# Modulation weights asked for three steps ahead, sums of squares as column strips, and the rotary key's tile two places earlier

## The chip, the cores and the metric

The kernel runs on one core of a Trainium2 chip. The metric is the device time of one execution in microseconds (us); several executions are timed, and the median is compared.

## The reference, cut to what matters

One decoder layer over 1024 tokens of width 1024 in float32: six modulation vectors from a condition vector, an input projection, latent attention beside a gated recurrence, an output projection, and a routed expert network of 32 experts. What the change touches is the modulation and the three latents of the input projection.

```python
mod = jax.nn.silu(c) @ w_ada + b_ada                      # 1024 -> 6 * 1024
shift1, scale1, gate1, shift2, scale2, gate2 = jnp.split(mod[:, None, :], 6, axis=-1)
h = rms_norm(x, norm1_g) * (1.0 + scale1) + shift1
proj = h @ w_in
q_lat, kv_lat, k_rope, x_lru, g_lru = jnp.split(proj, IN_SPLITS, axis=-1)
attn = mla_attention(q_lat, kv_lat, k_rope, ...)          # rms_norm(q_lat) @ w_q_b, rms_norm(kv_lat) @ w_kv_b
lru = rg_lru_branch(x_lru, g_lru, ...)                    # conv, two gates, a scan, times gelu(g_lru)
mixed = jnp.concatenate([rms_norm(attn, ...), rms_norm(lru, ...)], axis=-1)
x = x + gate1 * (mixed @ w_out)
h2 = rms_norm(x, norm2_g) * (1.0 + scale2) + shift2
x = x + gate2 * hierarchical_moe(h2, ...)
```

## The kernel before

The program is one stream that a scheduler orders at build time: engines take their instructions in the order that its timeline gives, and the code fixes pieces of that order with added dependencies (`ordered`, `add_manual_dep`). Each engine and each DMA queue then works strictly in its own order. SP is the queue of nearly all loads.

Big tiles come from one pool: tag `b` (`blk`, 128x1024, 41 slots) and tag `h` (`half`, 128x512, 12 slots). A load is issued when its slot is free, and everything behind it on SP waits with it.

The front of the layer runs to about 250 us. `FT` (L50) lists the twelve column tiles of the input projection: `kl` and `ql` are the latents, `xl` the recurrence's input, `kr` the rotary key, `gl` the gelu branch. Each tile's weights are split into a high and a low part, and each product is three matmuls (L225, L226, L227) of 128x512 into a bank `pp` (three banks); a `kr` tile has 64 columns, and both parts side by side, in two matmuls (L537, L538). The first three tiles (`k1` is 3) run half by half while the rows of x are normed and turned (L376, tiles `pt`, then `xT` on ACT, `hTh` and `hTl`); the others follow one by one. After a tile's half, `evac` takes the bank: `lat_k` and `lat_q` copy a latent and call `sq_cols` (L600), `conv` makes four ACT and DVE steps, `k_rope` sums the squares of the rotary key and turns it. `gate_mm` and `gate` (L563, L573) make the two gates of an `xl` tile, with tables changed on ACT between sigmoid, exp, tanh and sqrt.

`sq_cols` squares a half (128 features x 512 tokens, `sqq`) on ACT, and TensorE sums over the features: each 128 columns of `sqq` are the stationary operand and a column of ones the moving one (L605, 128x1), so that tokens land on partitions (`pc`), and DVE copies four columns into `ssq`.

`ada` (L483) makes the four later modulation vectors in sixteen steps, eight for each of two groups: a step loads 128 rows of `w_ada` as four tiles `wad` of 128x512 (L490) and runs four matmuls of 32x512 (L494), which stand on four strips of 32 columns of the array. The first of the four waits for all four loads, and the four stay together. After eight steps the bias is loaded (`adab`), added to the bank `pm`, and the result goes to DRAM (`mod_d`, L512) and from there to `m_g1`, with which POOL scales `wo`. The steps are handed out between the tiles of the projection (`next(ag)` after each four products). `modulate` (L439) does the same for the first two vectors, from 128x256 tiles (L445), at the start.

From there on attention runs head by head (to about 500 us), then the router and the experts, whose weights `ew` are 186 loads of 512 KB, issued as slots come free.

Of the kernel before, what the change touches and what calls it, by code (L numbers as in the profile page):

```python
# [14 lines left out]
AF = mybir.ActivationFunctionType  # L15
# [5 lines left out]
D = 1024  # L21
S = 1024
NT = 8
# [22 lines left out]
for _n, _w in ROWS:  # L46
    ROFF[_n] = (_o, _w)
    _o += _w
NROW = _o
FT = [("kl", 0), ("ql", 0), ("xl", 0), ("ql", 1), ("xl", 1), ("xl", 2), ("xl", 3), ("kr", 0),  # L50
      ("gl", 0), ("gl", 1), ("gl", 2), ("gl", 3)]
GE = 8
FRONT = [8 * g + i for i in range(2) for g in range(4)]
# [47 lines left out]
for _n, _w in GRP:  # L101
# [2 lines left out]
NGRP = _o  # L104
OPT = {
# [33 lines left out]
def layer(ctx, tc, A, out, dbg=None, stop=None):  # L139
    nc = tc.nc  # L140
    V, SC, G, T, SY = nc.vector, nc.scalar, nc.gpsimd, nc.tensor, nc.sync
# [8 lines left out]
    def blk(name, dt=F32):  # L150
        return big.tile([128, 1024], dt, name=name, tag="b", bufs=NBLK)

    def half(name, dt=F32):
        return big.tile([128, 512], dt, name=name, tag="h", bufs=NHALF)
# [11 lines left out]
    def bank(name):  # L166
        ph = OPT["ph"][cur["n"]]
        tg = ph["tags"][name]
        return cur["ps"].tile([128, 512], F32, name=name, tag=tg, bufs=ph["n"][tg])
# [59 lines left out]
    def t3(ap, t):  # L229
        return ap.rearrange("p (t f) -> p t f", t=t)  # L230
# [5 lines left out]
    xs, last = {}, {}  # L236
# [9 lines left out]
    def load_in(i):  # L246
        if i >= len(FT):
            return
        kind, j = FT[i]
        M = 64 if kind == "kr" else 128  # L250
        f0 = FCOL[kind] + j * 128
        w = blk("win")
        v = t3(w, 8)[:, :, :M]
        SY.dma_start(v, A["w_in"][:, f0:f0 + M].rearrange("(k p) f -> p k f", p=128))
        wraw[i] = v
# [64 lines left out]
    ones_f = const.tile([128, 128], F32, name="ones_f")  # L320
# [3 lines left out]
    ident = const.tile([128, 128], F32, name="ident")  # L324
# [11 lines left out]
    ones_c = ones_f[:, 0:1]  # L336
# [9 lines left out]
    cs32 = const.tile([128, 8, 32], F32, name="cs32")  # L346
# [134 lines left out]
    mc = {g: const.tile([128, 16], F32, name=f"mc{g}") for g in (1, 2)}  # L481

    def ada():  # L483
        for g in (1, 2):
            pm = bank("pm")
            for k in range(8):
                ws, ld = [], []
                for i in range(4):
                    w = half("wad")
                    ld.append(SY.dma_start(w, A["w_ada"][k * 128:(k + 1) * 128, g * 2048 + i * 512:g * 2048 + (i + 1) * 512]).ins)  # L490
                    ws.append(w)
                with ordered(T):
                    for i in range(4):
                        m = T.matmul(pm[32 * i:32 * i + 32, :], cs32[:, k, :], ws[i], start=(k == 0), stop=(k == 7),  # L494
                                     skip_group_check=True).ins
                        if i == 0:
                            for d in ld[1:]:
                                tc.add_manual_dep(m, d.name, mybir.DependencyInfo(
                                    mybir.DependencyClass.Sync, mybir.DependencyReason.DATA), reason="four at once")
                yield  # L500
            bt = half("adab")
            for i in range(4):
                b = A["b_ada"]
                SY.dma_start(bt[32 * i:32 * i + 32, :],
                             bass.AP(tensor=b.tensor, offset=b.offset + g * 2048 + i * 512, ap=[[0, 32], [1, 512]]))
            V.tensor_add(bt, bt, pm)
            pmc = bank("pmc")
            for c in range(4):
                T.matmul(pmc[:, c:16:4], bt[:, c * 128:(c + 1) * 128], ident[:, 0:128:32], start=True, stop=True)
            V.tensor_copy(mc[g], pmc[:, :16])  # L510
            for i in range(4):
                G.dma_start(mod_d[g * 2048 + i * 512:g * 2048 + (i + 1) * 512], bt[32 * i:32 * i + 1, :])  # L512
# [83 lines left out]
    ssq = const.tile([128, 3, NT], F32, name="ssq")  # L596
# [3 lines left out]
    def sq_cols(pp, n, j):  # L600
        sq = half("sqq")
        SC.activation(sq, pp, AF.Square)
        pc = bank("pc")
        for t in range(4):
            T.matmul(pc[:, t:t + 1], sq[:, t * 128:(t + 1) * 128], ones_c, start=True, stop=True)  # L605
        V.tensor_copy(ssq[:, j, n * 4:n * 4 + 4], pc[:, :4])

    def lat_q(i, n):
        j = FT[i][1]
# [21 lines left out]
    def k_rope(i, n):  # L631
        pp = hold.pop(i)
        if n == 0:
            lq["kr"] = blk("krT")
        kr = lq["kr"]
        SC.activation(kr[:, NS[n]], pp, AF.Copy)
        if n == 1:
            i2 = half("ident2")[:, :64]
            V.tensor_add(i2, ident[:, :64], ident[:, 64:])
            pk = bank("pk")  # L640
            for t in range(NT):
                T.matmul(pk[:, t * 64:(t + 1) * 64], kr[:, t * 128:(t + 1) * 128], i2, start=True, stop=True)
            kb = blk("kb")
            sqr, tmp = t3(kb[:, :512], NT), t3(kb[:, 512:], NT)
            with tc.issue_after(last["hi"]):
                SC.activation(sqr, t3(pk, NT), AF.Square)
            V.tensor_reduce(ssr, sqr, op=OP.add, axis=AX.X)
            rope(krr, t3(pk, NT), NT, "k", 0, tmp)

# [17 lines left out]
    ag = ada()  # L667
# [40 lines left out]
    lx, le, ld, l2, lp = (const.tile([128, 4], F32, name=n) for n in ("lx", "le", "ld", "l2", "lp"))  # L708
# [23 lines left out]
    SY.dma_start(rsti, bass.AP(tensor=A["pos_r"].tensor, offset=A["pos_r"].offset, ap=[[0, 128], [1, S]]))  # L732
    load_in(K1)
    load_in(K1 + 1)
    for i in range(8):
        kind, j = FT[i]
        if i >= K1:
            load_in(i + 2)
            split_in(i + 1)
            if i == 7:  # L740
                split_in(i + 2)
        if kind == "xl":
            load_gate(j)
        for n in range(2) if i >= K1 else (1,):
            for _ in project(i, n) if i >= K1 else ():
                for _ in range(OPT["adv"]):
                    next(ag, None)
            if n == (0 if i >= K1 else 1):
                gates()
            if (i, n) == (7, 1):  # L750
                wk = blk("wk")
                SY.dma_start(wk, A["w_kv_b"])
                wkh, wkl = blk("wkh", F32R), blk("wkl", F32R)
                last["hi"] = SC.activation(wkh, wk, AF.Copy).ins
                V.tensor_sub(wkl, wk, wkh)
            evac(i, n)
        if i < K1:
            wsp.pop(i)
        if i == 1:
            split_in(K1)  # L760
            V.tensor_scalar(rst, rsti, 0, None, op0=OP.is_equal)
            V.tensor_scalar(rcap, rst, -1.0, 2.0, op0=OP.mult, op1=OP.add)
        if kind == "xl":
            pend.append(j)
# [913 lines left out]
    for n, u in enumerate(UNITS):  # L1678
# [14 lines left out]
        pg = gate_up(u, X.pop(n), mid)  # L1693
# [81 lines left out]
```

## Time and profile before

| | us |
|---|---|
| median of 3 runs | 809.95 (808.85 to 810.82) |
| the profiled execution's own time | 816.49 |
| its span, first to last instruction | 814.6 |
| TensorE busy | 728.1 (89%) |
| VectorE busy | 447.2 (55%) |
| ScalarE busy | 317.0 (39%) |
| GpSimd busy | 157.6 (19%) |

The profiled execution is 6.5 us above the median, and what lies around its span is 1.9 us. Shares of the whole span mix stages with different limits: up to 500 us TensorE is busy nearly all the time and the DMA engines about half of it, and behind that it is the DMA engines that are full. A wait that TensorE has in the front is therefore read from the front alone.

### The profile page before, as it was taken

What the parts mean: (1) busy time and instruction counts of PE and PEld (TensorE: products, weight loads), DVE (VectorE), ACT (ScalarE), POOL (GpSimd) and SP (SyncE); (2) the same over time, 40 slices, a digit from 0 to 9 for tenths busy, and PEclk for the clock granted to TensorE, in tenths of its full rate; (3) what the DMA queues carried; (4) which work ended last, traced back from release to release, by engine and by line L of the source; (5) the groups of instructions that cost most, each with busy time, mean ns of one, the idle gap of its engine ahead of it and who ended that gap; (6) DMA issues with size and microseconds to landing.
All of it is one profiled execution on the core that took longest, in us unless ns stands there. A gap on an engine that the chain in (4) does not pass through costs nothing. (4 is left out here: it accounts for less than half of the span.)

```text
span 814.6 us, 12260 instructions
## 1 busy us (share of the span) xinstructions
PE 728.1 (89%) x4257; PEld 471.2 (58%) x4257; DVE 447.2 (55%) x1334; ACT 317.0 (39%) x715; POOL 157.6 (19%) x150
## 2 busy tenths in 40 slices
PE   3899999989988989899999997699979899999874
PEld 1477776548877878788888886333333343332321
DVE  4597386868777469797884667344334222213210
ACT  3455456666354157667664434121201211102200
POOL 1121012103665102031311000212112112212010
PEclk9989999999999999999999998699989999999998
DMA  9952437681317403020154789999999999999994
GB/s 311 372 151 84 143 108 236 210 280 58 109 44 259 168 39 104 1 79 1 54 173 144 259 311 343 346 316 349 313 373 330 329 335 336 369 347 354 304 320 102
DMA packets 70976, 180.47 MB, mean 222 GB/s; under 512 B 8960, under 2 KB 22528, under 8 KB 70912
## 3 DMA queue, kind: packets, MB, share of 16 engines
q1 hardware_dynamic: 63328, 158.50, 55.1%
q0 software_dynamic: 7104, 21.00, 9.5%
q8 instruction: 34, 0.56, 0.3%
q10 hardware_dynamic: 480, 0.16, 0.2%
q14 instruction: 30, 0.25, 0.1%
HBM read 160.61 MB, written 22.95 MB: 225 GB/s over the span
## 5 line engine op out<-in xcount | busy, mean ns | idle before, releaser
L1649 PE MATMUL pgu<-ew,xeT 128*32 128x512 f32 (+1 forms) x928 | 163.4, 613 | 8.1 <-DMA ew<-in_w_e 7.3
L1649 PEld LDWEIGHTS pgu<-ew,xeT 128*32 128x32 f32 (+1 forms) x928 | 48.3, 121 | 99.4 <-issue 79.0
L1660 PE MATMUL py<-ew,hT 128*32 128x512 f32 (+1 forms) x464 | 75.1, 597 | 5.8 <-ACT hT L1634 5.8
L225 PE MATMUL pp<-hTh,winh 128*128 128x512 f32 x176 | 69.2, 406 | 5.8 <-DVE hTh L188 3.0
L226 PE MATMUL pp<-hTl,winh 128*128 128x512 f32 x176 | 71.1, 404 | 0.0
L227 PE MATMUL pp<-hTh,winl 128*128 128x512 f32 x176 | 70.4, 401 | 0.0
L1663 DVE TENSOR_TENSOR y<-py,m_g 128x512 f32<-128x512 f32 (+1 forms) x40 | 27.5, 691 | 69.3 <-PE py L1660 64.3
L1623 ACT ACTIVATE sg<-pgu 128x256 f32<-128x256 f32 (+1 forms) x20 | 7.7, 387 | 142.9 <-PE pgu L1649 135.8
L1660 PEld LDWEIGHTS py<-ew,hT 128*32 128x32 f32 (+1 forms) x464 | 23.5, 120 | 48.3 <-issue 35.7
L1616 DVE TENSOR_SCALAR xeT<-pxe,gc,mc 128x128 f32<-128x128 f32 x80 | 27.4, 404 | 33.0 <-PE pxe L1610 33.0
L225 PEld LDWEIGHTS pp<-hTh,winh 128*128 128x128 f32 x176 | 34.0, 194 | 16.3 <-DVE hTh L188 4.0
L1665 POOL DMA_INDIRECT out<-y,pki x13 | 20.7, 1589 | 111.2 <-DVE y L1663 87.7
L1625 DVE SCALAR_TENSOR_TENSOR hid<-sg,pkw,pgu 128x256 f32<-128x256 f32 (+1 forms) x13 | 6.2, 479 | 63.4 <-ACT sg L1623 60.9
L1634 ACT ACTIVATE hT<-pht 128x256 f32<-128x256 f32 (+1 forms) x20 | 7.6, 380 | 85.1 <-PE pht L1632 65.4
L1614 ACT ACTIVATE xeT<-pxe,mc,gc 128x128 f32<-128x128 f32 x80 | 30.0, 461 | 24.9 <-PE pxe L1610 24.9
L226 PEld LDWEIGHTS pp<-hTl,winh 128*128 128x128 f32 x176 | 33.9, 193 | 9.9 <-issue 2.1
L227 PEld LDWEIGHTS pp<-hTh,winl 128*128 128x128 f32 x176 | 34.1, 194 | 8.6 <-issue 1.7
L949 ACT ACTIVATE P<-pS,nb,scq 128x384 f32<-128x384 f32 (+2 forms) x48 | 32.3, 679 | 12.2 <-DVE nb L946 12.2
L983 PE MATMUL po<-PT,v 128*128 128x256 f32 (+1 forms) x160 | 35.8, 362 | 0.0
L1046 POOL TENSOR_TENSOR wo<-wo,m_g 128x256 f32<-128x256 f32 x32 | 28.2, 916 | 15.3 <-DMA wo<-in_w_out 15.3
L983 PEld LDWEIGHTS po<-PT,v 128*128 128x128 f32 x160 | 28.8, 191 | 2.9
L1610 PEld LDWEIGHTS pxe<-ident,xe 128*128 128x128 f32 x160 | 18.2, 145 | 20.7 <-issue 14.4
(424 smaller groups left out, 1613.6 us busy)
## 6 DMA issues: line engine op xcount, KB each, us to landing
ew<-in_w_e SPq DMA_DIRECT2D x186, 512.0 KB
wad<-in_w_ada SPq DMA_DIRECT2D x64, 256.0 KB
wada<-in_w_ada SPq DMA_DIRECT2D x16, 512.0 KB
win<-in_w_in SPq DMA_DIRECT2D x12, 512.0 KB
xt<-in_x SPq DMA_DIRECT2D x8, 512.0 KB
wo<-in_w_out SPq DMA_DIRECT2D x8, 512.0 KB
xr<-in_x SPq DMA_DIRECT2D x8, 512.0 KB
x_d<-xr SPq DMA_DIRECT2D x8, 512.0 KB
```

What stands on the lines that cost most here:

```text
L225: T.matmul(o, lhi, rhi, start=first, stop=False)
L226: T.matmul(o, lhi, rlo, start=False, stop=False)
L227: T.matmul(o, llo, rhi, start=False, stop=last)
L949: SC.activation(Pt[:, o:o + w], pss[ci], AF.Exp, scale=P["scq"][:, i:i + 1], bias=nb, accum_out=l[:, ci:ci + 1])
L983: T.matmul(po[:, o:], P["v"][:, js], PT[j // 4][:, j % 4, o:], start=(j == 0), stop=(j == nj - 1), skip_group_check=True)
L1046: EN[OPT["g1"]].tensor_mul(w[:, q:q + 256], w[:, q:q + 256], mrow["g1"][:, q:q + 256])
L1614: SC.activation(xT[a][:, c], pt[:, c], AF.Identity, scale=gc[:, k:k + 1], bias=sh2[:, k:k + 1])
L1616: last["dve"] = V.tensor_scalar(xT[a][:, c], pt[:, c], gc[:, k:k + 1], sh2[:, k:k + 1], op0=OP.mult, op1=OP.add).ins
L1649: T.matmul(pg[r], xT[k // 4][:, c + r.start:c + r.stop], w[k // 2][:, NS[k % 2]], start=(k == 0), stop=(k == 7), skip_group_check=True)
L1660: T.matmul(py[n][r], hT[:, a * 128 + r.start:a * 128 + r.stop], w[4 + a][:, NS[n]], start=(a == 0), stop=(a == 1), skip_group_check=True)
L1663: last["dve"] = V.tensor_mul(y[:rows, NS[n]], py[n][:rows], mrow["g2"][:rows, NS[n]]).ins
L1665: G.indirect_dma_start(out=out, out_offset=bass.IndirectOffsetOnAxis(ap=idx, axis=0), in_=y[r0:r0 + idx.shape[0]], in_offset=None, compute ...
```

## The change

Three edits, and the order that the scheduler then finds.

- `ada` loads a step's weights as two tiles of 128x1024 from tag `b` in place of four of 128x512 from tag `h`. Three steps are asked for at the start (a `next(ag)` ahead of the fourth tile), and each step asks for the step three behind it, after its matmuls. The matmuls are the same 64, on halves of the two tiles; the first of a step waits for both loads.
- `sq_cols` swaps the operands: 32 columns of ones are stationary and 128 columns of `sqq` move, four times, on four strips of the array, so that a strip holds 32 equal rows of sums for 128 tokens. ACT copies the bank to `sqr`, TensorE transposes it (bank `pct`, of the two banks E), and DVE takes every 32nd column.
- In `FT` the `kr` tile stands sixth, ahead of the last two `xl` tiles, and its square on ACT has no order set any more.

```diff
@@ -47,7 +47,7 @@
     ROFF[_n] = (_o, _w)
     _o += _w
 NROW = _o
-FT = [("kl", 0), ("ql", 0), ("xl", 0), ("ql", 1), ("xl", 1), ("xl", 2), ("xl", 3), ("kr", 0),
+FT = [("kl", 0), ("ql", 0), ("xl", 0), ("ql", 1), ("xl", 1), ("kr", 0), ("xl", 2), ("xl", 3),
       ("gl", 0), ("gl", 1), ("gl", 2), ("gl", 3)]
 GE = 8
 FRONT = [8 * g + i for i in range(2) for g in range(4)]
@@ -104,7 +104,7 @@
 NGRP = _o
 OPT = {
     "ph": [
-        {"tags": {"pp": "A", "pt": "C", "pg": "C", "pkv": "C", "pq": "C", "pm": "D", "pL": "A", "pc2": "E", "pm2": "E", "pmc": "E", "pc": "E",
+        {"tags": {"pp": "A", "pt": "C", "pg": "C", "pkv": "C", "pq": "C", "pm": "D", "pL": "A", "pc2": "E", "pm2": "E", "pmc": "E", "pc": "E", "pct": "E",
                   "pk": "E", "ptq": "E", "ptk": "E", "ptk2": "E"}, "n": {"A": 3, "C": 2, "D": 1, "E": 2}},
         {"tags": {"pS": "A", "ptP": "A", "po": "D", "pkv": "E", "pq": "E", "ptq": "E", "ptk": "E", "ptk2": "E", "pc2": "E",
                   "pth": "A", "pr": "D", "pA": "A", "ppos": "B", "pbr": "B", "ptab": "B"}, "n": {"A": 4, "D": 1, "E": 2, "B": 1}},
@@ -481,22 +481,34 @@
     mc = {g: const.tile([128, 16], F32, name=f"mc{g}") for g in (1, 2)}
 
     def ada():
+        asked = []
+
+        def ask(n):
+            if n < 16:
+                g, k = n // 8 + 1, n % 8
+                ws = []
+                for c in range(2):
+                    w = blk("wad")
+                    o = g * 2048 + c * 1024
+                    ws.append((w, SY.dma_start(w, A["w_ada"][k * 128:(k + 1) * 128, o:o + 1024]).ins))
+                asked.append(ws)
+
+        for n in range(3):
+            ask(n)
+        yield
         for g in (1, 2):
             pm = bank("pm")
             for k in range(8):
-                ws, ld = [], []
-                for i in range(4):
-                    w = half("wad")
-                    ld.append(SY.dma_start(w, A["w_ada"][k * 128:(k + 1) * 128, g * 2048 + i * 512:g * 2048 + (i + 1) * 512]).ins)
-                    ws.append(w)
+                ws = asked.pop(0)
                 with ordered(T):
                     for i in range(4):
-                        m = T.matmul(pm[32 * i:32 * i + 32, :], cs32[:, k, :], ws[i], start=(k == 0), stop=(k == 7),
+                        w = ws[i // 2][0][:, (i % 2) * 512:(i % 2) * 512 + 512]
+                        m = T.matmul(pm[32 * i:32 * i + 32, :], cs32[:, k, :], w, start=(k == 0), stop=(k == 7),
                                      skip_group_check=True).ins
                         if i == 0:
-                            for d in ld[1:]:
-                                tc.add_manual_dep(m, d.name, mybir.DependencyInfo(
-                                    mybir.DependencyClass.Sync, mybir.DependencyReason.DATA), reason="four at once")
+                            tc.add_manual_dep(m, ws[1][1].name, mybir.DependencyInfo(
+                                mybir.DependencyClass.Sync, mybir.DependencyReason.DATA), reason="four at once")
+                ask(g * 8 - 8 + k + 3)
                 yield
             bt = half("adab")
             for i in range(4):
@@ -600,10 +612,15 @@
     def sq_cols(pp, n, j):
         sq = half("sqq")
         SC.activation(sq, pp, AF.Square)
-        pc = bank("pc")
+        pc = bank("pc")[:, :128]
         for t in range(4):
-            T.matmul(pc[:, t:t + 1], sq[:, t * 128:(t + 1) * 128], ones_c, start=True, stop=True)
-        V.tensor_copy(ssq[:, j, n * 4:n * 4 + 4], pc[:, :4])
+            T.matmul(pc[32 * t:32 * t + 32], ones_f[:, :32], sq[:, t * 128:(t + 1) * 128], start=True, stop=True,
+                     skip_group_check=True)
+        sr = half("sqr")[:, :128]
+        SC.activation(sr, pc, AF.Copy)
+        pct = bank("pct")
+        T.transpose(pct[:, :128], sr, ident)
+        V.tensor_copy(ssq[:, j, n * 4:n * 4 + 4], pct[:, 0:128:32])
 
     def lat_q(i, n):
         j = FT[i][1]
@@ -642,8 +659,7 @@
                 T.matmul(pk[:, t * 64:(t + 1) * 64], kr[:, t * 128:(t + 1) * 128], i2, start=True, stop=True)
             kb = blk("kb")
             sqr, tmp = t3(kb[:, :512], NT), t3(kb[:, 512:], NT)
-            with tc.issue_after(last["hi"]):
-                SC.activation(sqr, t3(pk, NT), AF.Square)
+            SC.activation(sqr, t3(pk, NT), AF.Square)
             V.tensor_reduce(ssr, sqr, op=OP.add, axis=AX.X)
             rope(krr, t3(pk, NT), NT, "k", 0, tmp)
 
@@ -732,6 +748,7 @@
     SY.dma_start(rsti, bass.AP(tensor=A["pos_r"].tensor, offset=A["pos_r"].offset, ap=[[0, 128], [1, S]]))
     load_in(K1)
     load_in(K1 + 1)
+    next(ag)
     for i in range(8):
         kind, j = FT[i]
         if i >= K1:
```

The order of instructions is the same in both kernels up to the first sums of squares (about 58 us in the trace) and, but for a few neighbours, from about 250 us on. Three places between:

ACT at the end of the first halves of the first three tiles, before: `xT` are the turned rows of x for the second halves, and `sqq` the squares of the first two latents.

```order
L221 ACTIVATE latkh<-pp,col 128x512
L613 ACTIVATE latq<-pp,col 128x512
L602 ACTIVATE sqq<-pp 128x512 x2
L552 ACTIVATE xr<-pp 128x512
L553 ACTIVATE xc<-pp,col 128x512
L467 ACTIVATE xT<-pt,modc,sc_260 128x512 x5
```

And there now (`sqr` is the copy of the sums' bank):

```order
L221 ACTIVATE latkh<-pp,col 128x512
L630 ACTIVATE latq<-pp,col 128x512
L614 ACTIVATE sqq<-pp 128x512
L564 ACTIVATE xr<-pp 128x512
L565 ACTIVATE xc<-pp,col 128x512
L620 ACTIVATE sqr<-pc 128x128
L614 ACTIVATE sqq<-pp 128x512
L620 ACTIVATE sqr<-pc 128x128
L467 ACTIVATE xT<-pt,modc,sc_260 128x512 x2
```

The second square and the two copies stand between `xc` and the first `xT`; before, `xT` followed `xc` at once.

TensorE at the last matmuls of the first three tiles and the first of the fourth, now: `wad` are the modulation's weights. Before, the same stretch has matmuls of `pp` alone, and the first `wad` stands 50 matmuls later in the row, where every run of `wad` is a whole step (x4).

```order
L506 MATMUL pm<-wad,cs_157 32x512 x6
L225 MATMUL pp<-hTh,winh 128x512 x3
L506 MATMUL pm<-wad,cs_157 32x512 x3
L226 MATMUL pp<-hTl,winh 128x512
L227 MATMUL pp<-hTh,winl 128x512
L226 MATMUL pp<-hTl,winh 128x512
L227 MATMUL pp<-hTh,winl 128x512
L226 MATMUL pp<-hTl,winh 128x512
L227 MATMUL pp<-hTh,winl 128x512
L506 MATMUL pm<-wad,cs_157 32x512 x7
L225 MATMUL pp<-hTh,winh 128x512
```

Four steps stand here as runs of 6, 3 and 7. Further on there is a run of 1 and 3, and one of 1 and 11; the other steps are whole, in runs of 4 or 8. There are 14 runs in all, before 16, and the last of them stands 56 matmuls earlier in the row than before.

SP in the middle of the modulation's loads, before (`gw` are gate weights, `win` a projection tile, `adab` the bias):

```order
L490 DMA wad<-in_w_ada 128x512 x9
L254 DMA win<-in_w_in 128x8x64
L490 DMA wad<-in_w_ada 128x512 x7
L260 DMA gw<-in_lru_wa 128x128
L260 DMA gw<-in_lru_wx 128x128
L504 DMA adab<-in_b_ada 32x512 x4
L490 DMA wad<-in_w_ada 128x512 x8
```

And now:

```order
L493 DMA wad<-in_w_ada 128x1024 x8
L254 DMA win<-in_w_in 128x8x128
L493 DMA wad<-in_w_ada 128x1024 x4
L260 DMA gw<-in_lru_wa 128x128
L260 DMA gw<-in_lru_wx 128x128
L516 DMA adab<-in_b_ada 32x512 x4
L493 DMA wad<-in_w_ada 128x1024 x4
```

The bias of the first group now stands behind the loads of thirteen of the sixteen steps; before, it stood behind those of eight.

## Rows read from the trace of the kernel before

**Rows 1.** The page's second part, 40 equal slices of the span, busy tenths.

```profile
PE   3899999989988989899999997699979899999874
...
DMA  9952437681317403020154789999999999999994
```

**Rows 2.** Stretches: time, busy us (instructions) of PE, PEld, DVE, ACT, POOL, PEclk, DMA share, GB/s.

```profile
170.00:180.00 10.00, 10.00 (x44) 6.30 (x43) 6.57 (x5) 8.58 (x9) 0.00 (x0) 0.83 0.95 314
650.00:700.00 50.00, 49.15 (x210) 20.19 (x209) 12.27 (x27) 7.71 (x22) 9.99 (x8) 1.00 1.00 347
```

**Rows 3.** What PE waited for, 38 to 250 us: us in total, times, longest.

```profile
PE pm L494 <- DMA wad<-in_w_ada: 3.3, 3, 2.1
...
PE pp L225 <- ACT xc L553: 1.6, 1, 1.6
...
PE pp L225 <- ACT krT L636: 0.8, 1, 0.8
```

**Rows 4.** Timeline of PE, 160 to 184 us: start, us, what [idle before].

```profile
161.84 1.06 PE L494 MATMUL pm<-wad,cs 128*32 128x512 f32 x8
...
168.75 1.06 PE L494 MATMUL pm<-wad,cs 128*32 128x512 f32 x8 [2.10 <-DMA wad<-in_w_ada]
...
170.45 0.63 PE L226 MATMUL pp<-hTl,winh 128*128 128x512 f32 x1
...
173.73 0.40 PE L225 MATMUL pp<-hTh,winh 128*128 128x512 f32 x1
173.96 0.39 PE L226 MATMUL pp<-hTl,winh 128*128 128x512 f32 x1
```

**Rows 5.** What SP's queue waited for, 40 to 180 us.

```profile
SPq L490 <- PE pm L494: 18.2, 8, 4.6
SPq L490 <- DVE gws L219: 16.3, 4, 8.2
```

**Rows 6.** Timeline of PE, 12 to 38 us, the first modulation: 128x256.

```profile
32.52 0.62 PE L445 MATMUL pm<-wada,cs 128*32 128x256 f32 x2
...
35.43 0.64 PE L445 MATMUL pm<-wada,cs 128*32 128x256 f32 x8
35.99 0.50 PE L226 MATMUL pp<-hTl,winh 128*128 128x512 f32 x1
```

**Rows 7.** Timeline of PE, 91 to 97 us: one whole step of later modulation.

```profile
90.96 0.39 PE L226 MATMUL pp<-hTl,winh 128*128 128x512 f32 x1
91.28 1.06 PE L494 MATMUL pm<-wad,cs 128*32 128x512 f32 x8
92.27 0.50 PE L227 MATMUL pp<-hTh,winl 128*128 128x512 f32 x1
92.61 0.39 PE L225 MATMUL pp<-hTh,winh 128*128 128x512 f32 x1
```

**Rows 8.** Tile wad: duration ns min/median/max, first and last start.

```profile
L494 PE MATMUL pm<-wad,cs x128: 589/593/617, 91.3 to 179.6; 128*32 128x512 f32 x128
```

**Rows 9.** Timeline of PE at the sums of squares, 58 to 62 us.

```profile
57.83 1.03 PE L376 MATMUL pt<-ident,xt 128*128 128x128 f32 x8
58.70 1.84 PE L605 MATMUL pc<-ones_f,sqq 128*128 128x1 f32 x16
60.41 0.64 PE L376 MATMUL pt<-ident,xt 128*128 128x128 f32 x4
60.80 0.94 PE L225 MATMUL pp<-hTh,winh 128*128 128x512 f32 x3
```

**Rows 10.** Timeline of ACT, 50 to 130 us, at the first sums.

```profile
57.15 1.09 ACT L602 ACTIVATE sqq<-pp 128x512 f32<-128x512 f32 x2 [3.75 <-DVE latkl L222]
...
58.60 0.79 ACT L553 ACTIVATE xc<-pp,col 128x512 f32<-128x512 f32 x1
59.26 1.47 ACT L467 ACTIVATE xT<-pt,modc,sc 128x512 f32<-128x512 f32 x2
```

**Rows 11.** Timeline of PE, 36 to 62 us: a matmul behind an ACT copy of 128x256.

```profile
38.23 0.61 PE L451 MATMUL pm<-ident,mrow 128*128 128x4 f32 x4 [0.50 <-ACT mrow L448]
```

## The prediction

> **What bounds the kernel now.** I read the slices of the span first. TensorE is busy in nearly every slice up to the 24th (some 490 us), while the DMA engines are full only in the first and from the 23rd on [rows 1]; late in the expert stage they are at 1.00 with 347 GB/s [rows 2]. So the front, up to 250 us, is bound by TensorE and by what it waits for, and the last 300 us by the expert weights' loads. These loads are asked for as attention and the experts free slots, in an order that the change leaves alone. What the front gains or loses should therefore reach the end whole: it moves the start of a queue that is full, not its length.
>
> Then the front's waits, by what ended them: 3.3 us for the weights `wad` in three waits, 1.6 us for ACT's copy `xc`, 0.8 us for `krT` [rows 3]. The longest, 2.10 us, has a second price: behind it TensorE runs at half clock. From 170.45 to 173.73 stand eight matmuls in 3.28 us, where the pitch then falls to 0.23 [rows 4]; at 0.23 they take 1.84, so 1.4 us were lost. The stretch has a granted clock of 0.83 [rows 2], a mean of the two levels, 1.2 and 2.4 GHz. Why `wad` came late shows in the loading queue: its loads stood 18.2 us for TensorE and 16.3 us for DVE's gate split to give back a slot of the small tag `h` [rows 5].
>
> All sums below are differences in the profiled execution (span 814.6, own time 816.49), which I set against the median of 809.95.
>
> **The change part by part.**
>
> *The loads.* Half as many, twice as large, in slots of the big tag, three steps ahead. They no longer stand behind gate tiles for a slot, so I take all three waits as gone: -3.3 us, and with the longest of them the half clock, -1.4. If tag `b` is as tight as `h` was, both are 0.
>
> *Where the steps stand now.* Since the first weights are there early, four steps are placed where TensorE waited 1.6 us for `xc` before [rows 3]. That wait is then filled: -1.6 us. It could at worst stay, 0.
>
> *Broken steps.* The four matmuls of a step stand on four strips and run side by side: one alone (two rows of the trace) lasts as long, 0.62, as four (eight rows), 0.64 [rows 6]. So a run of `wad` costs by the number of times that it comes back to a strip. Runs of 6, 3 and 7 cost five sets in place of four, 1 and 3 two in place of one, 1 and 11 four in place of three: three sets more. A whole set of 512 columns takes 0.99 from its start to the next start, and going in and out costs 0.09 and 0.11 over the pitch of 0.23 [rows 7]. Three sets are 3.0; two runs fewer (14 for 16) save 2 x 0.2. Net +2.6 us. If the broken pieces lie where TensorE would wait anyway, it is 0.
>
> *The sums.* Before, 16 rows of 128x1 take 1.71 for two calls, 0.86 each [rows 9], six calls 5.1, and some 0.1 each for going out. A strip set of 128 columns isn't in the trace. At 256 columns a set takes 0.56 [rows 6], at 512 0.99 [rows 7], so 0.21 for each 128, and 0.35 at 128; with 0.2 for going in and out 0.55. A transpose is 0.11 (eight in 0.87 [rows 9]), with 0.1 for standing alone 0.2. So 0.75 for a call, six calls 4.5 against 5.3 to 5.7: -0.8 us. The bounds: -1.6 if a set hides its edges, +0.5 if 128 columns take as long as 256.
>
> Rows 7 show those edges without saying what they are. The Trainium skill, "TensorEngine Tiling (Array Packing)", Tiling Modes, Key Properties, says that changing the tiling mode drains the engine; this speaks against strips that are put singly between full-width products. By the rows the six new visits pay 6 x 0.2, which is in the sum; were there no drain, the term would be -2.0.
>
> *The chain that the sums now make.* A call used to end on TensorE with a copy behind it on DVE. Now it goes TensorE, ACT, TensorE, DVE. Four of the six have other matmuls between the parts, which cover it. The first two have none: sums, transpose, sums, transpose in a row, and ACT does the second square only after the first copy. A hop through ACT left TensorE idle for 0.50 with a copy of 256 columns [rows 11]. Two hops, the second square (0.55, half of 1.09 [rows 10]), two sets and two transposes make about 2.4 where 1.71 stood. Behind it on ACT waits the first `xT`, which began at 59.26 right after `xc` [rows 10] and would begin at about 61; the matmul at 60.80 [rows 9] needs it through a DVE cast. TensorE has eight transposes to do meanwhile instead of four, some 0.4. I take +1.2 us, bounds 0.2 and 1.8.
>
> *The rotary key's tile.* The same matmuls, two places earlier; its ACT and DVE work goes with it. I cost the move at nothing, since what its 16 small products and its square fed is needed only by head 0. What covered the gates of the last `xl` tile, though, was this tile and the steps beside it. That cover is the price of the slower rival.
>
> *Six more copies on ACT*: ACT is off the path save in the chain above, so 0.
>
> Sum: -3.3 - 1.4 - 1.6 + 2.6 - 0.8 + 1.2 = **-3.3 us**, 806.6. What is late next are ACT's copies that free the `pp` banks, like the 0.8 for `krT` [rows 3]; I leave those waits as they are.
>
> **The rivals.**
>
> *The cover is gone (slower).* The last step stood at 179.6 [rows 8], beside the gates of the last `xl` tile; now the last one stands 56 matmuls earlier, and the gates of the last two tiles run without any. Before, four steps stood from 161.84 on [rows 4], each 1.19 with its edges [rows 7]. If TensorE waits for ACT's table changes and sigmoids where they lay, up to 4.8 us open, with another half clock of 1.4: -3.3 + 4.8 + 1.4 = +2.9, 812.9. It decides once more than 3.3 us, about 70% of the cover, lies open. For it: 0.8 us lay open there even with the steps. Against it: the gelu tiles' products follow, and the scheduler has put them between these gates. Chance 0.21.
>
> *The waits only move.* SP still works in one order, and the bias of the first group now stands behind thirteen steps' loads instead of eight; step nine can't start before that bias has been added and the bank is free. If slots of `b` come late, TensorE waits there what it waited for `wad`: 3.3 us back, about 809.9. Against it: from the eighth step to the ninth lie 70 matmuls, 16 us. Chance 0.22.
>
> *More than the sum.* The broken sets fill waits (0 for 2.6), the sums reach their lower bound (-1.6), the chain costs 0.2: -3.3 - 1.4 - 1.6 - 1.6 + 0.2 = -7.7, 802.2. For it: the scheduler breaks a step only where its own timeline shows a hole. Chance 0.12.
>
> **How the numbers follow.** The forecast has 0.45, with a range of its own of 804 to 808.5. A difference of 0.2%, 1.6 us, is about what a measurement of this kernel can tell from no change. Faster by more: nearly all of the forecast and the larger gain, 0.56. Within it: the moved waits and the forecast's edge, 0.23. Slower by more: 0.21. The range goes from the larger gain to the lost cover, 802.0 to 813.0, which leaves out about 2 in 10 with what no case has in it.
>
> **What would show it.** Loads: no wait of TensorE for `wad` over 0.5 us, and no half clock between 100 and 190 us. Placing: the first `wad` matmuls at about 79 us, and no wait for `xc` there. Broken steps: a run of one `wad` matmul that lasts as long as a run of three. Sums: a strip set of about 0.35 and a call of 0.75. Chain: transposes of x that follow the first sums about a microsecond late, and a wait of the next `pp` matmul for `hTh`. End: the first expert load, and the last instruction, earlier by what the front gained. I am wrong if tag `b` holds the loads back, if gates wait in the open behind 160 us, or if the end doesn't move with the front.

## The result and the profile of the changed kernel

The changed kernel takes 830.6 us (median, 826.0 to 835.1); before, on the same chip, 810.0. The ratio is 1.024, with a 95% interval from 1.020 to 1.028: slower by some 20 us, where 806.6 was forecast and 813 was the upper end of the range. The profiled execution has a span of 833.2 us.

The loss is made in the front and then carried through nearly unchanged. These are TensorE's first query products and the experts' first products, from the tile views of after (operation, count, duration, first and last start):

```profile
L837 PE MATMUL pq<-wq,latq x128: 323/326/402, 244.3 to 416.0; 128*128 128x192 f32 x128
```

```profile
L1666 PE MATMUL pgu<-ew,xeT x928: 589/592/1174, 540.3 to 818.3; 128*32 128x512 f32 x163, 128*128 128x512 f32 x23
```

Before, the first pq stood at 225.0 and pgu ran from 520.5 to 799.6. So 19.3 us are lost by the first pq, 19.8 by the first expert product, and 18.7 are left at the last. That the end moves with the front was right; the sign of what the front does was not.

TensorE's waits of after up to there, 62 to 244.3 us (total, times, longest), which answer to [rows 3]:

```profile
PE pp L225 <- ACT xc L565: 7.4, 1, 7.4
PE pkv L225 <- ACT gt_wx L583: 3.5, 1, 3.5
PE pp L227 <- DVE winl L277: 2.7, 1, 2.7
PE pp L225 <- ACT winh L276: 1.6, 1, 1.6
PE pp L225 <- ACT gelu L670: 1.3, 1, 1.3
PE pm L506 <- DMA wad<-in_w_ada: 0.8, 1, 0.8
```

They sum to 17.3 us; the same view of before sums to 7.1 up to 225 us. The wait for `wad` has gone from 3.3 to 0.8, nearly as forecast, but a single wait for ACT's copy `xc` costs more than all of before's. The second price stands behind the waits. TensorE's timeline of after there:

```profile
119.03 0.79 PE L225 MATMUL pp<-hTh,winh 128*128 128x512 f32 x1 [7.43 <-ACT xc L565]
...
122.61 0.54 PE L227 MATMUL pp<-hTh,winl 128*128 128x512 f32 x1
122.99 0.40 PE L225 MATMUL pp<-hTh,winh 128*128 128x512 f32 x1
```

After 7.43 us of idling nine products take 3.96 us, where nine pitches of 0.23 are 2.07. The granted clock of both stretches is a mix of 1.2 and 2.4 GHz, 0.80 and 0.85, where before had 1.00 (stretches as in [rows 2], of after):

```profile
110.00:120.00 10.00, 2.57 (x13) 1.17 (x12) 3.89 (x3) 9.92 (x13) 2.35 (x1) 0.80 0.36 111
120.00:130.00 10.00, 10.00 (x51) 6.25 (x50) 10.00 (x13) 5.21 (x8) 0.00 (x0) 0.85 0.39 121
```

Counted over all products of 512 columns that last over 0.53 us (43 in after, 8 in before), the pitch in excess of 0.23 sums to 9.4 us against 1.5. So waits (+10.2) and half clock (+7.9) make 18.1 of the 19.3 us. The half clock stands behind several of the waits: the granted clock is also 0.69 from 160 to 170 us and 0.79 from 170 to 180, behind those for `winh` and `winl`.

Why `xc` was late is in ACT's timeline. After:

```profile
92.78 0.28 ACT L620 ACTIVATE sqr<-pc 128x128 f32<-128x128 f32 x1 [3.48 <-PE pc L617]
92.95 0.59 ACT L614 ACTIVATE sqq<-pp 128x512 f32<-128x512 f32 x1
98.48 0.28 ACT L620 ACTIVATE sqr<-pc 128x128 f32<-128x128 f32 x1 [4.93 <-PE pc L617]
98.65 0.41 ACT L218 ACTIVATE gws<-gw 128x256 fp32r<-128x256 f32 x1
...
107.92 1.37 ACT L583 ACTIVATE gt_wa<-pg,col 128x512 f32<-128x512 f32 x2 [7.56 <-PE pg L227]
...
118.20 0.78 ACT L565 ACTIVATE xc<-pp,col 128x512 f32<-128x512 f32 x1
```

And before, at the same place in the program:

```profile
81.09 1.10 ACT L602 ACTIVATE sqq<-pp 128x512 f32<-128x512 f32 x2
82.05 0.46 ACT L218 ACTIVATE gws<-gw 128x256 fp32r<-128x256 f32 x1
...
89.56 0.69 ACT L571 ACTIVATE gt_wa<-pg,col 128x512 f32<-128x512 f32 x1 [4.01 <-PE pg L227]
```

Before, ACT does the two squares at once, then splits the gate weights `gws`. After, the second square and the split each stand behind a copy `sqr` that waits for TensorE's strips: 8.4 us of waiting in two copies. The gates of the first input tile follow 18 us later (89.56, 107.92), and their table changes and sigmoids then fill ACT from 107.92 to 117, just when it should empty the `pp` banks (`latq`, `xr`, `xc`). With three such banks TensorE stands.

### The profile page after: what moved, and what is told of

It reads as the page before. It is cut to its first block, busy times and chain, and to the rows that moved or that the text cites. A ratio compares the mean times of both kernels' runs of the same rounds, so it can differ in the third digit from the quotient of the medians.

```text
span 833.2 us, 12192 instructions
## 1 busy us (share of the span) xinstructions
PE 736.7 (88%) x4263; PEld 475.1 (57%) x4263; DVE 450.5 (54%) x1334; ACT 320.0 (38%) x722; POOL 156.7 (19%) x150
## 5 line engine op out<-in xcount | busy, mean ns | idle before, releaser
L225 PE MATMUL pp<-hTh,winh 128*128 128x512 f32 x176 | 73.1, 428 | 13.8 <-ACT xc L565 7.4
L227 PE MATMUL pp<-hTh,winl 128*128 128x512 f32 x176 | 72.5, 413 | 2.7 <-DVE winl L277 2.7
L226 PE MATMUL pp<-hTl,winh 128*128 128x512 f32 x176 | 74.0, 421 | 0.0
L226 PEld LDWEIGHTS pp<-hTl,winh 128*128 128x128 f32 x176 | 35.7, 203 | 11.2 <-issue 2.9
## 6 DMA issues: line engine op xcount, KB each, us to landing
wada<-in_w_ada SPq DMA_DIRECT2D x16, 512.0 KB, 10.8
```

What stands on the lines that cost most here:

```text
L225: T.matmul(o, lhi, rhi, start=first, stop=False)
L226: T.matmul(o, lhi, rlo, start=False, stop=False)
L227: T.matmul(o, llo, rhi, start=False, stop=last)
```

## The experiments

My first theory from this trace was the queue: the loads asked for early stand for slots of tag `b` at the head of SP's queue, and hold back the input and gate weights. Its rivals were the key tile's missing cover and a scheduler that spreads the loss over all edits. The four kernels of the first set decide that.

In the table each ratio is to runs of before on the same chip, whose medians lay at 812.7 to 813.7 us there; the last columns are the first gate product and the first pq of the profiled run (before: 88.7 and 225.0). One caution on the last column: the profiled run of before reaches its first sum of squares at 58.70 us, the others between 56.84 and 57.83, so a difference of 1 to 2 us to 225.0 can lie ahead of the change.

| kernel | us | ratio (95%) | first pg | first pq |
|---|---|---|---|---|
| ada_alone | 816.8 | 1.0044 (1.0014 to 1.0073) | 90.1 | 227.8 |
| kr_alone | 821.1 | 1.0093 (1.0064 to 1.0123) | 87.7 | 230.7 |
| sums_alone | 829.4 | 1.0189 (1.0136 to 1.0242) | 103.8 | 244.7 |
| kr_and_sums | 837.7 | 1.0297 (1.0245 to 1.0349) | 100.9 | 247.8 |
| sums_in_place | 809.1 | 0.9945 (0.9901 to 0.9988) | 87.5 | 222.2 |
| copy_and_slot | 831.8 | 1.0235 (1.0178 to 1.0292) | 103.5 | 243.3 |
| strips_copy_on_dve | 826.9 | 1.0189 (1.0133 to 1.0246) | 99.1 | 239.4 |
| sums_copy_in_b | 811.6 | 0.9974 (0.9947 to 1.0001) | 83.2 | 223.0 |
| extra_tile_no_wait | 814.1 | 1.0007 (0.9970 to 1.0044) | 87.6 | 223.5 |
| after_in_place | 819.5 | 1.0079 (1.0049 to 1.0109) | 94.9 | 224.6 |
| no_key_move | 820.6 | 1.0084 (1.0050 to 1.0118) | 92.4 | 228.8 |
| key_own_bank | 821.9 | 1.0122 (1.0064 to 1.0179) | 87.7 | 193.0 |
| key_without_dve | 817.1 | 1.0043 (1.0011 to 1.0075) | 87.5 | 227.9 |
| loads_one_ahead | 813.9 | 1.0010 (0.9983 to 1.0037) | 89.2 | 223.0 |
| sums_in_place_dve | 805.8 | 0.9940 (0.9908 to 0.9973) | 86.7 | 220.7 |
| sums_and_one_ahead | 812.2 | 0.9970 (0.9939 to 1.0001) | 89.8 | 221.1 |
| after_all_mended | 817.5 | 1.0048 (1.0015 to 1.0081) | 89.3 | 223.3 |

### Which edit

Each edit alone on the kernel before, and the changed kernel without the first edit; the diffs are the pieces of the change shown above.

> The kernel before with the first edit alone: later modulation's weights as whole blocks, asked for three steps ahead; sums and the order of the tiles as before. Queue theory (the loads asked for early wait for slots at the head of the one loading queue, and hold back the input weights behind them): 822 to 831 us, and the loads of the last xl tiles' weights are issued 10 us or more later than before. Cover theory (the rotary key's tile that left its place among the gates is the cause): 806 to 811 us, since that tile is not moved here. Scheduler theory (each edit shifts the order a little and the loss is the sum of all three): 812 to 820 us.

> The kernel before with the third edit alone: the rotary key's tile in front of the last two input tiles. Queue theory: 808 to 812 us, within a microsecond or two of before. Cover theory: 815 us or more, with waits of TensorE for gate tiles behind 160 us. Scheduler theory: 813 to 820 us.

> The kernel before with the second edit alone: the latents' sums of squares as column strips with a copy and a transpose. Queue theory and cover theory: 808 to 811 us, the terms -0.8 and +1.2 of the prediction nearly cancel. Scheduler theory, or a chain through ACT that costs more than thought: 813 us or more.

> The changed kernel with the first edit undone: small halves asked for at their step, in tag h, as before. Queue theory: 807 to 813 us, so the whole loss of some 20 us goes with this one edit. Cover theory: 820 to 831 us, the loss stays. Scheduler theory: 815 to 825 us.

As the cause of the whole loss the queue theory falls: the loads alone cost 0.4%, and without them the loss is larger, 1.0297, above every range set down for that kernel. The largest part are the sums, which the prediction had at -0.8 + 1.2: alone they cost 1.9%, with the first gate 15 us late. The key tile's move alone costs 0.9%. Each of the three costs something, as the scheduler theory has it, but they don't sum: alone they make 3.3%, together 2.4%.

### What in the sums

A call takes four new things: strips, a copy on ACT, a transpose, and a second tile of tag `h` for the copy. The next kernels separate them. The edits, in this order: the copy over the square's own tile; the old products with a copy on ACT into a tile of its own; the copy on DVE.

```diff
-        sr = half("sqr")[:, :128]
+        sr = sq[:, :128]
...
+        sr = half("sqr")[:, :4]
+        SC.activation(sr, pc[:, :4], AF.Copy)
-        V.tensor_copy(ssq[:, j, n * 4:n * 4 + 4], pc[:, :4])
+        V.tensor_copy(ssq[:, j, n * 4:n * 4 + 4], sr)
...
-        SC.activation(sr, pc, AF.Copy)
+        V.tensor_copy(sr, pc)
```

> The kernel before with the strips, the copy on ACT and the transpose, as in sums_alone, but the copy is written over the square's own first 128 columns, so that a call takes no second slot of tag h. Slot theory (the second tile of a call pushes the next square, the gate weights and so the first gates back): 808 to 813 us, the first gate's product at about 90 us. Copy theory (ACT stands in its order and waits for TensorE before each copy): 822 to 831 us, since the copy stays. Strip theory (mode changes and the transposes on TensorE): 822 to 831 us too.

> The kernel before with its 128x1 products as they were, but their four sums go through a copy on ACT into a tile of tag h before DVE takes them; no strips, no transpose. Slot theory: 820 to 831 us, nearly all of the loss of sums_alone. Copy theory: 820 to 831 us as well. Strip theory: 808 to 813 us.

> As sums_alone, with the copy on DVE in place of ACT, in its own tile of tag h. Slot theory: 820 to 831 us, first gate's product still behind 100 us. Copy theory: 808 to 814 us. Strip theory: 820 to 831 us.

> The changed kernel whole, with the copy over the square's own tile and no second slot of tag h. Slot theory: the changed kernel's 830.6 less some 12 to 18, so 812 to 819 us, still above before by what the rotary key's move costs. Copy theory and strip theory: 827 to 833 us, no change.

Only the tile separates the slow from the fast. The old products with a copy of four columns lose 2.35%; the strips with their copy and transpose, but without a tile of their own, gain 0.55%. ACT's timeline of sums_in_place has the old order back, the copy (here `sqq<-pc`) behind the gate weights:

```profile
81.14 1.10 ACT L602 ACTIVATE sqq<-pp 128x512 f32<-128x512 f32 x2
82.09 0.45 ACT L218 ACTIVATE gws<-gw 128x256 fp32r<-128x256 f32 x1
...
86.63 0.28 ACT L608 ACTIVATE sqq<-pc 128x128 f32<-128x128 f32 x1 [2.34 <-PE pc L605]
```

That ACT's wait for the copy is not the cause by itself is shown by strips_copy_on_dve, whose ACT does no copy. Its ACT, and under it its DVE:

```profile
81.03 0.62 ACT L602 ACTIVATE sqq<-pp 128x512 f32<-128x512 f32 x1
...
84.09 0.58 ACT L602 ACTIVATE sqq<-pp 128x512 f32<-128x512 f32 x1
84.57 0.41 ACT L218 ACTIVATE gws<-gw 128x256 fp32r<-128x256 f32 x1
100.47 1.28 ACT L571 ACT_TABLE_LOAD   x1 [15.50 <-PE pg L227]
```

```profile
91.92 0.29 DVE L608 COPY sqr<-pc 128x128 f32<-128x128 f32 x1
...
94.91 0.43 DVE L219 TENSOR_TENSOR gws<-gw,gws 128x256 fp32r<-128x256 f32 x1
```

Here ACT has the gate weights' high part at 84.57, yet it then waits 15.5 us for the gates' products, which start at 99.1. Their low part is split on DVE, and there it stands behind the second copy, at 94.91; before, DVE splits it at 83.49. So with the copy on either engine, the split of the gate weights is complete only behind a copy that waits for TensorE's sums. Two more kernels ask why: the copy's tile from tag `b`, and a further tile of tag `h` that waits for no product.

```diff
-        sr = half("sqr")[:, :128]
+        sr = blk("sqr")[:, :128]
...
         V.tensor_copy(ssq[:, j, n * 4:n * 4 + 4], pc[:, :4])
+        V.memset(half("sqr")[:, :4], 0.0)
```

> As sums_alone, with the copy's tile taken from the big tag b in place of the small tag h; the copy stays on ACT and the strips stay. Order theory (tag h hands its slots out in the order of the calls, so the second square and the gate weights stand behind a copy that waits for TensorE): 806 to 814 us, the first gate's product near 90 us. Tightness theory (any further tile in SBUF is too much at this place): 820 us or more, since b has no free slots to give away either. The first slot theory, which named only the tag, is silent on which of the two.

> The kernel before with its 128x1 products and one further tile of tag h in each call, written by DVE alone with zeros in four columns and read by nobody, so that it waits for no product. Order theory: 810 to 815 us, as before, since the further tile holds nothing up. Tightness theory: 820 us or more, as copy_and_slot.

Both are as fast as before. So it isn't that tag `h` is too tight for one more tile. A tile of `h` that waits for TensorE, asked for between the first square and the next user of `h`, is what costs. In all three slow kernels of this kind the instructions that write tiles of `h` keep the order of the calls on their engine: square, copy, square, copy, gate weights on ACT in sums_alone and copy_and_slot; in strips_copy_on_dve square, square, gate weights on ACT and copy, copy, gate weights on DVE. That the scheduler hands out a tag's slots in the order of the calls is inferred from this, not read; a thirteenth slot wasn't tried.

The changed kernel with the copy in place gets back two thirds of its loss, 1.0239 to 1.0079; its 819.5 us are at the upper edge of the slot theory's range.

### The key tile and the loads

key_own_bank gives `pkv` the banks of tag E; key_without_dve replaces `kr x (I_a + I_b)`, whose addition is on DVE, by two products; loads_one_ahead asks for a step's blocks one step ahead.

```diff
-"pkv": "C", "pq": "C",
+"pkv": "E", "pq": "C",
...
-            V.tensor_add(i2, ident[:, :64], ident[:, 64:])
-                T.matmul(pk[...], kr[...], i2, start=True, stop=True)
+                for a in range(2):
+                    T.matmul(pk[...], kr[...], ident[:, a * 64:a * 64 + 64], start=(a == 0), stop=(a == 1))
...
-        for n in range(3):
+        for n in range(1):
-                ask(g * 8 - 8 + k + 3)
+                ask(g * 8 - 8 + k + 1)
```

> As kr_alone, with the first head's key products (pkv) given the small work's two banks in place of the two that the gates' products use, so that they needn't wait for ACT to empty these. Cover theory (the gates of the last input tile lie open because no tile follows them, and the next products want their banks): 3.5 to 5 us less than kr_alone, 813 to 819 us, with no wait of pkv for gt_wx. Rival (the move costs through the loads or through DVE's work for the key tile): 819 to 824 us, as kr_alone.

> As kr_alone, with the key tile's turn made by two products per block against the identity's halves, 8 more products of 64 columns and no addition on DVE ahead of them. If the wait for DVE of 2.6 us and the half clock behind it are what the move costs: 3 to 4 us less than kr_alone, 814 to 818 us against a before of 813. If the move costs by its missing cover at the last gates: 819 to 823 us, as kr_alone.

TensorE's waits of kr_alone, 62 to 230 us, and under them those of key_own_bank, 62 to 236:

```profile
PE pkv L225 <- ACT gt_wx L571: 3.5, 1, 3.5
PE pk L642 <- DVE ident L639: 2.6, 1, 2.6
```

```profile
PE ptq L850 <- ACT qnp L823: 3.4, 1, 3.4
PE pq L819 <- DVE qtmp L834: 3.3, 1, 3.3
...
PE pq L819 <- ACT gt_wx L571: 2.4, 1, 2.4
```

One price of the move is shown. It is the wait of 2.6 us for an addition on DVE, and the half clock behind it: without it the time falls by 4 us of the 7.4. The other, the cover, is read from the waits and not shown: behind the last gates the first head's products want the banks that ACT's sigmoids still hold, 3.5 us, then 1.3 for `gelu`, but the kernel made to remove that wait, key_own_bank, is no faster, and its 821.9 us lie in the range set down for the rival. With banks of its own `pkv` no longer waits, the scheduler pulls pq forward to 193.0, and pq waits for the same sigmoids, 2.4, and what follows for `qnp`, 3.4: the wait only moves. The Trainium skill, "Perfetto Trace Analysis", Optimizing Tensor Performance, advises to let groups of matmuls rotate through different PSUM banks, so that emptying one overlaps the next; here that was worth nothing (1.0122 beside 1.0093), and by these rows TensorE then waited for the same ACT work.

> As ada_alone, with each step's two blocks asked for one step ahead instead of three. Queue theory (loads asked for early hold back the input weights): nearer to before, 810 to 815 us, the last two input tiles' weights issued earlier. If the blocks themselves or the broken steps cost the 3 us: 815 to 820 us, as ada_alone.

> The changed kernel with the rotary key's tile back at its old place, and the strips' copy on DVE over the square's own tile, so that no second slot of tag h is taken: what is left are the loads and the strips. If the key's tile costs as much here as alone (some 7 us) and the loads some 3: before less 4 for the sums plus 3, 809 to 815 us. If the loads cost nothing once the sums are mended: 804 to 810 us. If the key's move is not a cost beside the others: 818 us or more, as after_in_place.

> As sums_in_place, with the copy on DVE: no second slot of tag h and no copy on ACT. If ACT's copies cost what the prediction took for the chain (1.2 us at the first two sums): 0.5 to 1.5 us under sums_in_place, 806 to 811 us beside a before of 813. If not: the same as sums_in_place within a microsecond.

> Strips with DVE's copy over the square's own tile, blocks asked for one step ahead, the rotary key's tile at its old place. If the gains add: sums_in_place_dve less nothing to 2 us, 803 to 808 us beside a before of 813, and faster than both kernels. If the loads' early steps push back the gates as in no_key_move: 813 to 820 us.

> The changed kernel with all three findings mended: the strips' copy on DVE over the square's own tile, blocks asked for one step ahead, the key tile's turn without DVE's addition; the key tile stays at its new place. If the three parts are independent: sums_in_place_dve's 6 to 7 us under before, and 3 to 4 above for the key's tile, 809 to 812 us beside a before of 813. If the key tile's missing cover costs more once the steps are done earlier, as after_in_place suggests: 815 to 820 us.

One step ahead costs nothing that can be measured, three cost 0.4%; the two intervals overlap, so the difference between them isn't settled. The waits (ada_alone, 62 to 228 us; under it loads_one_ahead, 62 to 223) differ in the input weights' split `winl`; the wait for `krT` is larger in both than before's 0.8:

```profile
PE pp L227 <- DVE winl L277: 2.6, 2, 2.3
PE pp L225 <- ACT krT L648: 2.6, 1, 2.6
```

```profile
PE pg L226 <- DVE xcl L219: 2.2, 1, 2.2
PE pp L225 <- ACT krT L648: 2.2, 1, 2.2
```

A second difference is on the loading queue, and it is the queue theory on a small scale. The split of the gate weights on ACT, in ada_alone and under it in loads_one_ahead:

```profile
88.36 0.42 ACT L218 ACTIVATE gws<-gw 128x256 fp32r<-128x256 f32 x1 [2.73 <-DMA gw<-in_lru_wx]
```

```profile
82.35 0.45 ACT L218 ACTIVATE gws<-gw 128x256 fp32r<-128x256 f32 x1
```

With three steps ahead SP issues the gate weights' loads at 80.4 us, behind more loads of `wad`; with one at 73.7; before, at 62.0. In no_key_move ACT waits 2.2 us for these loads as well, and its first gate product stands at 92.4 where sums_in_place_dve has 86.7. No run changes this alone, so its share isn't known.

The parts do not add. The best is sums_in_place_dve, 0.6% faster than before; with one step ahead it is 0.3%, not settled from none, and its 812.2 us lie between the two ranges set down. The sums mended and three steps ahead (no_key_move) lose 0.8%, though the parts alone are -0.6 and +0.4. That is as much as after_in_place, which has the key tile's move too, so beside the three steps the move costs nothing that can be measured; with one step ahead it costs 0.8% (after_all_mended beside sums_and_one_ahead). And with all causes mended the whole change still loses 0.5%. Its waits from 62 to 230 us are these three:

```profile
PE pkv L225 <- ACT gt_wx L583: 3.4, 1, 3.4
PE pq L837 <- DVE qtmp L852: 2.9, 1, 2.9
PE pp L225 <- ACT gelu L670: 1.3, 1, 1.3
```

From 62 to 186 us TensorE there waits for nothing longer than 0.5 us. Then come the bare gates, 3.4 + 1.3, and half clock behind them (granted clock 0.70 from 190 to 200 us). Yet the loss isn't made there: behind all that the first pq stands at 223.3, no later than before's 225.0, even less the 1.2 us by which the run of before came late to its first sum. It is made in the first head. These are the stretches from the first pq to the second head's first `pkv`, after_all_mended and then before (as in [rows 2]):

```profile
223.30:295.60 72.30, 63.04 (x279) 51.99 (x278) 45.19 (x96) 23.00 (x58) 29.06 (x31) 0.91 0.36 132
```

```profile
225.00:289.90 64.90, 57.98 (x280) 48.37 (x278) 40.35 (x96) 21.87 (x57) 27.88 (x29) 0.97 0.39 146
```

The same products take 7.4 us more, with waits of 9.2 us for 6.9 and more half clock; the longest waits are 2.9 for DVE's turning of the queries (`qtmp`; before 1.5) and 2.5 for DVE's adding of the recurrence's output to the rows of x (`xr`; 1.0). after_in_place, too, is level at the first pq, and takes 68.1 us for this stretch. Why the first head suffers, why three steps ahead cost what one doesn't, and why the parts don't add, stays open.

## The prediction, point by point

**What bounds the front, and the end that follows it:** right; 19.3 us at the first pq, 18.7 at the last expert product. The kernels with the sums mended show that the first head can lose time too.

**Loads:** the wait for `wad` fell from 3.3 to 0.8, where no wait over 0.5 was to be left. The half clock of before at 170 us has given way to others, behind other waits, so the sign "no half clock between 100 and 190 us" failed. Placing: the first `wad` stands at 79.34, and the wait for `xc` there is gone, both as forecast. But alone the edit costs 0.4% where its terms summed to -3.7 us. The step that failed is "They no longer stand behind gate tiles for a slot, so I take all three waits as gone": gone they are, but other waits took their place.

**Broken steps:** right. One product of a step that was broken lasts as long as three (0.97 to the next start, and 0.99), from TensorE's timeline of after:

```profile
102.65 1.04 PE L506 MATMUL pm<-wad,cs 128*32 128x512 f32 x2
103.62 0.33 PE L622 MATMUL pct<-ident,sqr 128*128 128x128 f32 x1
103.88 1.06 PE L506 MATMUL pm<-wad,cs 128*32 128x512 f32 x6
104.87 0.50 PE L225 MATMUL pp<-hTh,winh 128*128 128x512 f32 x1
```

All runs of `wad`, to the next start and without waits, come to 18.4 us against 16.1: +2.3 for the +2.6 forecast.

**The sums:** a strip set was put at 0.35 and is 0.35, with 0.09 more going in and 0.11 going out, so the edges that [rows 7] show come with 128 columns too:

```profile
91.97 0.39 PE L226 MATMUL pp<-hTl,winh 128*128 128x512 f32 x1
92.29 0.43 PE L617 MATMUL pc<-sqq,ones_f 128*32 128x128 f32 x8
92.64 0.50 PE L227 MATMUL pp<-hTh,winl 128*128 128x512 f32 x1
92.98 0.39 PE L225 MATMUL pp<-hTh,winh 128*128 128x512 f32 x1
```

What the edit can be worth is sums_in_place_dve: 0.6%, some 5 us, where -0.8 and +1.2 for the chain were forecast. That is not the strips' own time: from the first sum to the first pq it takes 163.1 us, before 166.3, and of these 3.2 us 1.2 are smaller waits and 1.5 half clock that isn't there. The bound of -1.6 is itself too small by the prediction's own sum, which has -2.0 without edges.

**The chain of the first two sums:** the waits are where they were said to be, 0.85, 0.16, 0.46 and 0.34, but the term was too small. TensorE's timeline of after, from the first sum to the next `pp` product, and of sums_in_place:

```profile
56.98 0.43 PE L617 MATMUL pc<-sqq,ones_f 128*32 128x128 f32 x8
...
61.38 1.54 PE L225 MATMUL pp<-hTh,winh 128*128 128x512 f32 x3
```

```profile
57.83 0.42 PE L605 MATMUL pc<-sqq,ones_f 128*32 128x128 f32 x8
...
60.08 0.96 PE L225 MATMUL pp<-hTh,winh 128*128 128x512 f32 x3
```

It takes 4.40 us where before took 2.10 [rows 9]: +2.3, above the upper bound of 1.8, and behind it eight products at half clock cost 1.6 more. (By the clock that product is only 0.6 us later than before's, because this run reached the sums 1.7 us earlier.) With the copy in place it is 2.25 us, without half clock: the second sum there stands behind the transposes of x. copy_and_slot, which has the tile and no strips, takes 4.87. So here too it is the order that comes with the copy's tile.

**The copies on ACT:** this is the step by which the prediction fell: "ACT is off the path save in the chain above, so 0". As work on ACT the copies do cost nothing that can be measured: over a tile already held the edit gives 0.9945 with them on ACT and 0.9940 on DVE. What the term left out is the tile that each copy takes from tag `h`. With that tile, and the copy on either engine, the loss is 15 to 19 us (sums_alone 1.0189, strips_copy_on_dve 1.0189, copy_and_slot 1.0235): the split of the gate weights, which takes its tile from the same tag, comes behind a copy that waits for TensorE, and the first gates come 10 to 15 us late with it. In after that shows as 8.4 us of waiting on ACT in the two sums behind the first input tile. [rows 5] had shown that loads wait for slots of `h`, but want of slots isn't the price (extra_tile_no_wait, 1.0007). The sign was in the order of ACT's instructions at the first sums, where the changed kernel has the second square behind the first copy.

**The key tile's move,** "I cost the move at nothing": it costs 0.9% alone, about half of it by an addition on DVE that came late (2.6 us); that the rest is the cover isn't shown.

**The rivals:** "The cover is gone" named the place and nearly the size: up to 4.8 us open, and 3.5 + 1.3 are in after, in kr_alone and in after_all_mended (ratio 1.0048, some 4 us; 2.9 were forecast). That the sizes agree is luck in part: in after_all_mended these waits lie ahead of a first pq that isn't late, and its loss is made behind. The rival had the sign right but not the main cause. "The waits only move" is what key_own_bank and the loads do, though not where it was said, before the ninth step. "More than the sum" did not come: no kernel with the loads' edit was faster than before by more than can be measured.

## What to carry to other kernels

Before a small copy is costed at nothing, write down which tag its tile comes from and what is asked for from that tag, and done by that engine, behind it: if the copy waits for TensorE, all of these wait, or are planned, behind it. Write it over a tile that is already held, or take it from another tag. An engine that is 38% busy, as ACT is here, is on the path wherever it has to free the banks of the bound engine: in after the first gates came 18 us late on it, and up to the first query product TensorE's waits grew by 10.2 us in all and the half clock behind them by 7.9.

## What was not expected of the hardware

Half clock is a price of its own size: in after it is 7.9 us more beside 10.2 us more of waits, and kr_alone has some 3.4 us of it beside 10.8 of waits up to the first pq (before: 1.5 and 7.1). Not each wait is followed by it: behind the 1.6 us at 79 us of before the granted clock stays at 1.00, behind the 2.1 at 166 us it falls to 0.83 in the next 10 us [rows 2, 4]. What tells the two apart no run here shows.
